# A Mamba-2 and latent-attention trunk: a planner with a DMA queue, larger transposes, and the first block's x in column halves

## The chip, the cores and the metric

The kernel runs on one core of a Trainium2 chip. The metric is the device time in microseconds of one execution of the whole program. The engines are TensorE (PE, with its weight loads PEld), VectorE (DVE), ScalarE (ACT), GpSimd (POOL) and SyncE (SP), which issues nearly all DMAs. The 16 DMA engines move what SP and POOL issue.

## The reference

Two layers on 2048 tokens of width 1024, each a pre-RMSNorm mixer with a residual add, and a final RMSNorm. Cut to what matters:

```python
h = x                                            # (1, 2048, 1024) float32
hn = rms_norm(h, g_pre[0])
z, xBC, dt = split(hn @ w_in)                    # 2048, 2048 + 2*4*128, 32 columns
xBC = silu(causal_conv4(xBC)); xs, B, C = split(xBC)
dt = softplus(dt + dt_bias); A = -exp(A_log)
y = ssd_scan(xs, dt, A, B, C)                    # 32 heads of 64, 4 groups, state 128, chunks of 256
y = group_rms((y + D * xs) * silu(z)) * g_out
h = h + y @ w_out
ckv, k_rope = split(rms_norm(h, g_kv_in) @ w_dkv)             # 256 + 32 columns
k_nope, v = split(rms_norm(ckv, g_ckv) @ w_ukv)               # 16 heads, 64 + 64
cq, gate = split(rms_norm(h, g_pre[1]) @ mla_w_in)            # 384 + 1024 columns
q = rms_norm(cq, g_q) @ w_uq                                  # 16 heads, 64 + 32 (rotary)
o = causal_softmax(q k^T) v
h = h + (o * silu(gate)) @ mla_w_out
return rms_norm(h, g_final)
```

## The kernel before

The tokens are tiled in four blocks of 512. A product of two float32 numbers is made of three products of 16-bit (or rounded 32-bit) halves, so each matrix product is issued as three matmuls per 128 rows of the contraction, into 128x512 banks of PSUM. The halves come from a copy on ACT and a subtraction on DVE.

The work comes in three stages.

1. **Mamba and MLA's projections** (to about 1960 us). `mamba` loads the constants `c_pack` (tile `pack`, 128x646, its first 128 columns the identity, behind it the gains), then block 0 of x (`load_x`: four tiles `hx` of 128x1024), squares it on ACT for the row scale (`rows_rms`, output `yt` with its sum `ms`), transposes it on PE against the identity, and splits it (`prep`: tiles `xT`, scaled by gains in `pack`). `steps` makes dt (tiles `big`, the dt chain on DVE, with the row scale `r`), `xbc` the conv inputs of a group of heads (first B and C, then the values `xs`), with weights loaded raw (`wraw`, three buffers) and split (`wsp`). Blocks 1 to 3 and MLA's blocks go through `prep16`, which scales x, splits it in 16-bit halves in `wsp` and transposes them by DMA (`DMA_TRANSPOSE xT<-wsp`, 128x8x128: eight squares of 128x128 in one). The residual is kept in `h_d` in DRAM, with tiles `hs`. MLA's part has for each block `mla_kv_down` and `mla_cq`, whose latents `turned` transposes by DMA, two squares at a time (tiles `BC` and `yT`), `mla_up` and `mla_gate`.

   All of that is not issued as it is written. It is recorded in a `Score`: each instruction with a cost from `cost()` (time on its engine, and time until its result is there), its dependencies (`graph`) and its tiles. `plan()` makes a list schedule from the front (`forward`: each engine takes, of what is ready, what has the best rank; eight DMAs of SP in flight at most), then one from the back (`backward`), which gives the ranks of the next turn, and keeps the plan with the earliest end. `play()` issues the instructions in that order. So costs and due times set the order of every engine, and also which buffer a tile gets. In the profile all these instructions stand at one line, L878 (L887 after).

2. **Attention** (about 1960 to 2600 us). `heads` issues 64 steps (head by block) from an order made by a planner with written tables, `Pace`. While it works on the last block, it begins the output product of block 0: for each of eight k, tasks G (loads of output, gate and reciprocal sums, `load_gated`, into a staging tile `os`), H (two DVE steps, L2260 and L2262), I (ACT copy of the upper half), J (DVE subtraction for the lower half, L2327) and P (products with `W`, L904 to L906). `GATED` is the number of staging tiles, `ASKED` at which of the 64 steps which k is begun.

3. **Output** (`back`, to the end). For blocks 1 to 3 the same by k in `gated`: loads into `os`, L2260, L2262, the copy to `oT` (L2466) and the subtraction (L2467). Then `residual` (L2481), `final` (L2487) and the stores.

Of the kernel before, what the change touches and what calls it, by code (L numbers as in the profile page):

```python
# [46 lines left out]
GATED = 2  # L47
ASKED = {61: (0,), 62: (1,), 63: (2, 3, 4, 5, 6)}
# [474 lines left out]
class Score:  # L523

    def __init__(self, nc, blank, name):
        self.ops, self.owns, self.rings = [], [], {}
# [103 lines left out]
    def graph(self):  # L630
# [201 lines left out]
    def plan(self):  # L832
# [48 lines left out]
class Net:  # L881
# [665 lines left out]
    def load_x(self, b, src, tag="hx"):  # L1547
# [1069 lines left out]
```

## Time and profile before

| | us |
|---|---|
| median of 3 runs | 2784.39 (2779.01 to 2787.86) |
| the profiled execution | 2791.74 |
| its span, first to last instruction | 2789.9 |
| PE busy | 2737.9 (98% of the span) |
| DVE, ACT, POOL busy | 2220.0, 1864.2, 675.6 |
| mean granted clock of PE | 0.994 |

In a row of the timeline or of the groups, `ps<-K,xT` reads output from inputs by the program's names; the numbers are start and length in us, and brackets hold the idle time before with what ended it. A granted clock of 1.00 is full speed. Busy PE is PE with a matmul in its array, at whatever clock.

### The profile page before, as it was taken

What the parts mean: (1) busy time and instruction counts of PE and PEld (TensorE: products, weight loads), DVE (VectorE), ACT (ScalarE), POOL (GpSimd) and SP (SyncE); (2) the same over time, 40 slices, a digit from 0 to 9 for tenths busy, and PEclk for the clock granted to TensorE, in tenths of its full rate; (3) what the DMA queues carried; (4) which work ended last, traced back from release to release, by engine and by line L of the source; (5) the groups of instructions that cost most, each with busy time, mean ns of one, the idle gap of its engine ahead of it and who ended that gap; (6) DMA issues with size and microseconds to landing.
All of it is one profiled execution on the core that took longest, in us unless ns stands there. A gap on an engine that the chain in (4) does not pass through costs nothing. (4 is left out here: it accounts for less than half of the span.)

```text
span 2789.9 us, 48569 instructions
## 1 busy us (share of the span) xinstructions
PE 2737.9 (98%) x16120; PEld 1550.7 (56%) x16120; DVE 2220.0 (80%) x5048; ACT 1864.2 (67%) x4914; POOL 675.6 (24%) x832
## 2 busy tenths in 40 slices
PE   7999999999999999999999999999999999999998
PEld 6888766554555555555555545454555555555443
DVE  5889899999988879888786564646889888889676
ACT  6889877877776667666655453334888888888322
POOL 0000000000000000000002121324888888888200
PEclk9999999999999999999999999999999999999999
DMA  5333456768668655586567987976999999999894
GB/s 178 98 113 105 118 178 220 215 204 256 187 187 256 175 141 178 160 243 185 145 186 232 292 236 210 250 197 183 181 189 183 186 203 198 190 200 185 209 278 153
DMA packets 687904, 535.88 MB, mean 192 GB/s; under 512 B 496642, under 2 KB 538626, under 8 KB 687652
## 3 DMA queue, kind: packets, MB, share of 16 engines
q1 hardware_dynamic: 674500, 490.16, 69.4%
q0 software_dynamic: 13152, 42.61, 5.1%
q8 instruction: 127, 2.08, 0.3%
q14 instruction: 125, 1.02, 0.1%
HBM read 307.57 MB, written 108.66 MB: 149 GB/s over the span
## 5 line engine op out<-in xcount | busy, mean ns | idle before, releaser
L878 PE MATMUL ps<-xT,wsp 128*128 128x512 f16 (+2 forms) x2416 | 567.7, 386 | 8.7 <-DVE wsp L878 6.0
L878 PE MATMUL ps<-wsp,xT 128*128 128x512 f16 (+3 forms) x2304 | 464.4, 358 | 1.9 <-DVE Sp L878 1.2
L2356 ACT ACTIVATE Pr<-ps,nm 128x512 f32<-128x512 f32 (+3 forms) x640 | 394.5, 628 | 83.7 <-DVE nm L2351 78.1
L2345 DVE TENSOR_REDUCE mx<-ps 128x1 f32<-128x512 f32 (+3 forms) x640 | 366.4, 604 | 54.1 <-PE ps L2311 45.9
L878 PEld LDWEIGHTS <-wsp 128*128 128x128 f16 x2448 | 234.0, 98 | 281.2 <-issue 21.6
L2362 POOL TENSOR_TENSOR HL<-Pr,HL 128x512 f16<-128x512 f32 x320 | 372.6, 1164 | 25.6
L878 PE MATMUL ps<-wsp,yT 128*128 128x512 f16 (+1 forms) x1536 | 356.7, 385 | 1.0 <-DVE rb L878 0.6
L878 POOL DMA_DIRECT2D gate_d<-xs x24 | 13.8, 590 | 1115.4 <-DVE kn L878 1101.3
L878 PEld LDWEIGHTS <-xT 128*128 128x128 f16 x1920 | 185.7, 98 | 166.5 <-issue 6.2
L904 PE MATMUL ps<-K,xT 96*128 96x512 f16 (+3 forms) x640 | 223.0, 348 | 2.9 <-ACT Pr L2356 1.8
L906 PE MATMUL ps<-K,xT 96*128 96x512 f16 (+3 forms) x640 | 221.9, 347 | 0.0
L905 PE MATMUL ps<-K,xT 96*128 96x512 f16 (+3 forms) x640 | 221.8, 347 | 0.0
L2361 POOL CAST HL<-Pr 128x512 f16<-128x512 f32 x320 | 196.6, 614 | 91.7 <-ACT Pr L2356 91.5
L878 DVE SCALAR_TENSOR_TENSOR cacc<-craw,pack,cacc 128x512 f32<-128x512 f32 x288 | 211.4, 746 | 4.6 <-ACT cacc L878 4.1
L878 PEld LDWEIGHTS <-yT 128*128 128x128 f16 x1152 | 110.2, 98 | 129.2 <-issue 3.8
L878 ACT ACTIVATE big<-big,d_cum 128x128 f32<-128x128 f32 x512 | 168.5, 393 | 8.8 <-DMA big<-cumT 8.8
L878 PE MATMUL ps<-xT,st 128*128 128x512 f16 x672 | 154.8, 382 | 3.7 <-DMA st<-w_d 3.7
L2375 ACT ACTIVATE PH<-ps 128x512 f16<-128x512 f32 (+3 forms) x320 | 143.4, 484 | 14.1 <-PE ps L2370 13.3
L2397 PE MATMUL ps<-PX,xT 128*64 128x512 f16 (+1 forms) x640 | 146.2, 383 | 1.6 <-DMA PX<-HL 1.2
L2397 PEld LDWEIGHTS <-xT 128*128 128x128 f16 (+1 forms) x1280 | 95.4, 103 | 91.4 <-issue 15.4
L2356 ACT ACTIVATION_READ_ACCUMULATOR Pr<-ps,nm 128x1 f32 x640 | 133.8, 209 | 0.0
L2370 PE MATMUL ps<-pack,Pr 128*128 128x128 f32 x896 | 133.4, 274 | 0.3 <-ACT Pr L2356 0.3
(380 smaller groups left out, 5348.3 us busy)
## 6 DMA issues: line engine op xcount, KB each, us to landing
wsp<-w_d SPq DMA_DIRECT2D x68, 512.0 KB, 3.9
wraw<-in_ssm_w_in_dram SPq DMA_DIRECT2D x128, 256.0 KB, 3.2
big<-cumT SPq DMA_DIRECT2D x64, 512.0 KB, 4.2
wraw<-in_ssm_w_out_dram SPq DMA_DIRECT2D x64, 256.0 KB, 3.3
w_d<-wsp SPq DMA_DIRECT2D x32, 512.0 KB, 4.3
wsp<-wo_d SPq DMA_DIRECT2D x32, 512.0 KB, 4.3
st<-w_d SPq DMA_DIRECT2D x56, 256.0 KB, 3.7
wsp<-wu_d SPq DMA_DIRECT2D x28, 512.0 KB, 4.2
```

The costliest lines, as they stand in the source:

```text
L878: call(*[self.real(x) for x in args], **{k: self.real(x) for k, x in named.items()})
L904: mm(out, l_hi, r_hi, start=start, stop=False)
L905: mm(out, l_hi, r_lo, start=False, stop=False)
L906: mm(out, l_lo, r_hi, start=False, stop=stop)
L2345: v.tensor_reduce(m[:, at:at + 1], s, AX.X, ALU.max, negate=True)
L2356: nc.scalar.activation(tile("Pr", n, j, c)[:, :w], bank("S", n, j, c)[:, :w], AF.Exp, bias=moves[(4 * n + j) % len(moves)], accum_out=sums ...
L2361: nc.gpsimd.tensor_copy(u[:, 0], x)
L2362: nc.gpsimd.tensor_tensor(u[:, 1], x, u[:, 0], ALU.subtract)
L2370: nc.tensor.transpose(bank("T", n, k)[:, j * P:(j + 1) * P], tile("Pr", n, j, k // 4)[:, k % 4 * P:(k % 4 + 1) * P], self.ident)
L2375: nc.scalar.activation(tile("PH", n, k)[:, c], bank("T", n, k)[:, c], AF.Copy)
L2397: nc.tensor.matmul(o, weights, half(n, k, low), start=start, stop=not left[n][at[0]])
```

## The change

No matmul is added, removed or altered. There are five parts:

- **The planner's model of DMAs.** A transpose was 1.4 us of issue and 3.3 until it lands, outside any queue; a copy went through a queue of 260 bytes per ns. Now both go through one queue (`wires`: 545 ns + bytes/288 for a transpose, 102 + bytes/359 for a copy), and `LATE`, added to each, is 600 for 1000 ns. The pass from the back has a queue too, and `FAR`, 1800 ns, per transfer. With `EARLY`, no row of SP is planned more than 30 us before it is due. 16 turns for 12. `links` are extra order edges.
- **Larger transposes.** `turned` transposes kv_down's latent of 256 in one DMA of four squares per 128 tokens instead of two of two; cq's 384 in one of four and one of two instead of three of two. Over four blocks there are 48 instead of 80.
- **The first block.** The identity is loaded first and the rest of `pack` behind four half tiles of x; x comes in eight DMAs of 128x512; the four squares on ACT are linked behind the fourth copy of `prep`.
- **Attention's end.** Four staging tiles for two (the new ones in parts of `K[0]` and of held tiles that are free by then), k = 0 and 1 begun at step 62 instead of 61 and 62, and H planned 7.5 instead of 5.5 us behind G.
- **The output stage.** Five buffers `os` for three.

```diff
-GATED = 2
-ASKED = {61: (0,), 62: (1,), 63: (2, 3, 4, 5, 6)}
+GATED = 4
+ASKED = {62: (0, 1), 63: (2, 3, 4, 5, 6)}
...
-                self.at(self.now + 5500, lambda k: self.ready["DVE"].append(("H", k, 0)), k)
+                self.at(self.now + 7500, lambda k: self.ready["DVE"].append(("H", k, 0)), k)
...
-PLANS = 12
+PLANS = 16
+EARLY = 30000
...
             if named.get("transpose"):
-                return 1400, 3300
-            issue = 700 if engine == "POOL" else 400
-            return issue, -moved
+                self.wires[len(self.ops)] = 545 + moved / 288
+                return 1300, 2470 + moved / 276
+            self.wires[len(self.ops)] = 102 + moved / 359
+            return 700 if engine == "POOL" else 400, 2000 + moved / 276
...
+        for m, n in self.links:
+            if all(m != k for k, _ in preds[n]):
+                preds[n].append((m, False))
...
-    SLACK, LATE = dict(DVE=40, ACT=40), 1000
+    SLACK, LATE, FAR = dict(DVE=40, ACT=40), 600, 1800
...
-        est = [0.0] * len(ops)
+        est = [max(0.0, due + rank[n] - EARLY) if o[0] == "SP" else 0.0 for n, o in enumerate(ops)]
...
-            if took < 0:
-                dma = max(dma, t) - took / 260
-                took = max(dma, t + 1900 - took / 160) - t + self.LATE
+            if n in self.wires:
+                dma = max(dma, t + 500) + self.wires[n]
+                took = max(took, dma + 1690 - t) + self.LATE
...
-            back[n] = t
...
+            if n in self.wires:
+                wire = max(wire + self.wires[n], t)
+                t = max(t, wire)
+            back[n] = t
...
-                if took_m < 0:
-                    took_m = 2400 - took_m / 150
-                elif f == "SP":
-                    took_m += 800
+                if m in self.wires:
+                    took_m += self.FAR
...
+            due = end if i > 1 else 0.0
...
-        nc.sync.dma_start(self.pack, self.a["c_pack"])
+        for cs in (slice(0, P), slice(P, PACK)):
+            nc.sync.dma_start(self.pack[:, cs], self.a["c_pack"][:, cs])
+        ops = self.score.ops
         self.load_x(0, self.a["x"][0:TB])
+        self.score.links += [(0, n) for n in range(2, 6)] + [(n, 1) for n in range(2, 6)]
+        squares = [n for n, o in enumerate(ops) if o[0] == "ACT"][:4]
...
+            if n == 0:
+                turned = [n for n in range(at, len(ops)) if ops[n][0] == "ACT"]
+                self.score.links += [(turned[3], n) for n in squares]
...
-        for i in range(4):
-            nc.sync.dma_start(xs[i], src[i * P:(i + 1) * P, :])
+        n = 1 if b else 2
+        for h in range(n):
+            cs = slice(h * D // n, (h + 1) * D // n)
+            for i in range(4):
+                nc.sync.dma_start(xs[i][:, cs], src[i * P:(i + 1) * P, cs])
...
-        out = [self.t(self.sp, tag, [P, 4, 2, P], F16, bufs=4) for _ in range(n)]
+        sets = [(k, m, self.t(self.sp, "yT" if m == 2 else "BC", [P, 4, 2 * m, P], F16, bufs=4))
+                for k, m in ((0, 2), (2, 1))[:n - 1]]
...
-            for k in range(n):
-                nc.sync.dma_start(out[k][:, i], u[:, k].rearrange("p s c -> p (s c)"), transpose=True)
-        return out
+            for k, m, o in sets:
+                nc.sync.dma_start(o[:, i], u[:, k:k + m].rearrange("p k s c -> p (k s c)"), transpose=True)
+        return [o[:, :, 2 * j:2 * j + 2] for k, m, o in sets for j in range(m)]
...
-                s = self.t(sp, "os", [P, 3, TB], bufs=3)
+                s = self.t(sp, "os", [P, 3, TB], bufs=5)
```

What the planner makes of it is shown at three places. First the start of SP's queue (`hx` and `hs` are tiles of x). Before:

```order
L878 DMA pack<-in_c_pack_dram 128x646
L878 DMA hx_139<-in_x_dram 128x1024
L878 DMA hx_148<-in_x_dram 128x1024
L878 DMA hx_150<-in_x_dram 128x1024
L878 DMA hx_152<-in_x_dram 128x1024
L878 DMA wraw_154<-in_ssm_w_in_dram 128x8x32
L878 DMA wraw_156<-in_ssm_w_in_dram 128x2x128
L878 DMA wraw_158<-in_ssm_w_in_dram 128x2x128
L878 DMA hs_160<-in_x_dram 128x1024
L878 DMA hs_169<-in_x_dram 128x1024
L878 DMA hs_182<-in_x_dram 128x1024
L878 DMA hs_202<-in_x_dram 128x1024
```

After:

```order
L887 DMA pack<-in_c_pack_dram 128x128
L887 DMA hx_141<-in_x_dram 128x512
L887 DMA hx_148<-in_x_dram 128x512
L887 DMA hx_150<-in_x_dram 128x512
L887 DMA hx_152<-in_x_dram 128x512
L887 DMA pack<-in_c_pack_dram 128x518
L887 DMA wraw_155<-in_ssm_w_in_dram 128x8x32
L887 DMA hx_141<-in_x_dram 128x512
L887 DMA hx_148<-in_x_dram 128x512
L887 DMA wraw_160<-in_ssm_w_in_dram 128x2x128
L887 DMA hx_150<-in_x_dram 128x512
L887 DMA hx_152<-in_x_dram 128x512
```

The four `hs` loads, and four `hx` of block 1 that came behind them, are gone from here; weights follow instead. On DVE at the same place, the subtractions that finish the weights of B and C (`wsp`, eight of 128x256) and the dt chain (`big`). Before, the chain's last part, with the third to sixth subtraction in it and behind it:

```order
L878 TENSOR_TENSOR wsp_365<-wraw_251,wsp_365 128x256
L878 TENSOR_SCALAR big_330<-big_330 128x128
L878 TENSOR_TENSOR big_330<-big_330 128x128
L878 TENSOR_TENSOR wsp_370<-wraw_287,wsp_370 128x256
L878 TENSOR_SCALAR big_330<-big_330 128x128
L878 TENSOR_TENSOR wsp_380<-wraw_299,wsp_380 128x256
L878 TENSOR_TENSOR big_330<-big_330 128x128
L878 SCALAR_TENSOR_TENSOR d_dt_399<-big_330 128x128
L878 TENSOR_TENSOR big_330<-d_dt_399,pack 128x128
L878 TENSOR_TENSOR wsp_412<-wraw_378,wsp_412 128x256
```

After, the last two of the eight and the head of the chain:

```order
L887 TENSOR_TENSOR wsp_340<-wraw_292,wsp_340 128x256
L887 TENSOR_TENSOR rss_365<-rsy_357 128x4
L887 SCALAR_TENSOR_TENSOR rsq_370<-rsx_335,rss_365 128x4
L887 TENSOR_TENSOR wsp_359<-wraw_305,wsp_359 128x256
L887 SCALAR_TENSOR_TENSOR rsy_375<-rsq_370,rsy_357 128x4
L887 TENSOR_TENSOR rss_380<-rsy_375 128x4
L887 SCALAR_TENSOR_TENSOR rsq_383<-rsx_335,rss_380 128x4
L887 SCALAR_TENSOR_TENSOR rsy_388<-rsq_383,rsy_375 128x4
L887 COPY r_106<-rsy_388 128x4
L887 TENSOR_SCALAR rh_107<-rsy_388 128x4
L887 SCALAR_TENSOR_TENSOR big_394<-ps_345,r_106,pack 128x32 x2
```

The chain's first step stood ahead of the third subtraction before; now it stands behind the eighth. Second, SP in MLA's first block, where the transposes of the next block's x (`xT<-wsp`) meet the residual (`h_d`, `hs`). Before:

```order
L878 DMA h_d<-hs_13842 128x1024
L878 DMA h_d<-hs_13855 128x1024
L878 DMA wsp_17563<-wu_d 128x1024
L878 DMA hs_17569<-h_d 128x1024
L878 DMA hs_17573<-h_d 128x1024
L878 DMA Xd_17579<-in_mla_w_out_dram 128x512
L878 DMA Xd_17589<-in_mla_w_out_dram 128x512
L878 DMA hs_17620<-h_d 128x1024
L878 DMA hs_17644<-h_d 128x1024
L878 DMA_TRANSPOSE xT_17407<-wsp_17614 128x8x128
L878 DMA_TRANSPOSE xT_17407<-wsp_17626 128x8x128
```

After:

```order
L887 DMA_TRANSPOSE xT_17322<-wsp_17301 128x8x128
L887 DMA_TRANSPOSE xT_17334<-wsp_17301 128x8x128
L887 DMA wsp_17347<-wu_d 128x2x1024
L887 DMA_TRANSPOSE xT_17322<-wsp_17314 128x8x128
L887 DMA_TRANSPOSE xT_17334<-wsp_17314 128x8x128
L887 DMA_TRANSPOSE xT_17322<-wsp_17272 128x8x128
L887 DMA wsp_17381<-wu_d 128x1024
L887 DMA_TRANSPOSE xT_17334<-wsp_17272 128x8x128
L887 DMA st_3157_17407<-w_d 128x1024
L887 DMA st_3160_17415<-w_d 128x1024
L887 DMA h_d<-hs_14129 128x1024
```

Six of the eight transposes now stand ahead of the first of these stores; the other two follow it, and the loads `hs` come behind all eight. Third, DVE in the output stage of block 1, where `final` of block 0 (the four wide `h`) meets the gates of k = 6 and 7. Before:

```order
L1338 SCALAR_TENSOR_TENSOR rsy_4128_29911<-rsq_4127_29909,rsy_4125_29905 128x4
L2487 SCALAR_TENSOR_TENSOR h_29804<-h_29804,rsy_4128_29911,gf 128x1024
L2487 SCALAR_TENSOR_TENSOR h_29805<-h_29805,rsy_4128_29911,gf 128x1024
L2487 SCALAR_TENSOR_TENSOR h_29806<-h_29806,rsy_4128_29911,gf 128x1024
L2487 SCALAR_TENSOR_TENSOR h_29807<-h_29807,rsy_4128_29911,gf 128x1024
L2260 TENSOR_TENSOR os_29921<-os_29921 128x512
L2260 TENSOR_TENSOR os_29931<-os_29931 128x512
L2262 SCALAR_TENSOR_TENSOR os_29921<-os_29921,us 128x512
L2262 SCALAR_TENSOR_TENSOR os_29931<-os_29931,us 128x512
L2467 TENSOR_TENSOR oT_29928<-os_29921,oT_29928 128x512
L2467 TENSOR_TENSOR oT_29938<-os_29931,oT_29938 128x512
```

After:

```order
L2492 TENSOR_TENSOR oT_29893<-os_29886,oT_29893 128x512
L1343 TENSOR_TENSOR rss_4115_29866<-rsy_4114_29864 128x4
L1345 SCALAR_TENSOR_TENSOR rsq_4116_29868<-rsx_4109_29854,rss_4115_29866 128x4
L1347 SCALAR_TENSOR_TENSOR rsy_4117_29870<-rsq_4116_29868,rsy_4114_29864 128x4
L1343 TENSOR_TENSOR rss_4118_29872<-rsy_4117_29870 128x4
L2281 TENSOR_TENSOR os_29896<-os_29896 128x512
L1345 SCALAR_TENSOR_TENSOR rsq_4119_29874<-rsx_4109_29854,rss_4118_29872 128x4
L2283 SCALAR_TENSOR_TENSOR os_29896<-os_29896,us 128x512
L1347 SCALAR_TENSOR_TENSOR rsy_4120_29876<-rsq_4119_29874,rsy_4117_29870 128x4
L2512 SCALAR_TENSOR_TENSOR h_29769<-h_29769,rsy_4120_29876,gf 128x1024
L2512 SCALAR_TENSOR_TENSOR h_29770<-h_29770,rsy_4120_29876,gf 128x1024
```

The gate of k = 6 (`oT_29893`) is whole ahead of the wide rows, and of k = 7 only the subtraction stands behind them.

More of the change, by code (lines that the diff above doesn't have):

```diff
@@ L693, in graph, with forward @@
             o.roots = [n for n in o.ops if not any(m in inside for m, _ in preds[n])]
-    SLACK, LATE = dict(DVE=40, ACT=40), 1000
+    SLACK, LATE, FAR = dict(DVE=40, ACT=40), 600, 1800
     HEAR = dict(PE=52, DVE=36, ACT=36, POOL=90, SP=60)
-    def forward(self, rank, order):
+    def forward(self, rank, order, due):
         ops, preds, succs, uses = self.ops, self.preds, self.succs, self.uses
         left = [len(p) + len(u) for p, u in zip(preds, uses)]
-        est = [0.0] * len(ops)
+        est = [max(0.0, due + rank[n] - EARLY) if o[0] == "SP" else 0.0 for n, o in enumerate(ops)]
         start = [0.0] * len(ops)
@@ L732, in forward @@
             if not k:
-                heapq.heappush(waiting[ops[n][0]], (0.0, n))
+                heapq.heappush(waiting[ops[n][0]], (est[n], n))
+                heapq.heappush(events, (est[n], ops[n][0]))
         for o in order:
@@ L796, in backward @@
         events = []
+        wire = 0.0
         for n, k in enumerate(left):
@@ L838, in plan @@
         order = sorted(self.owns, key=lambda o: o.first)
-        best = None
+        best, due = None, 0.0
         for i in range(PLANS):
-            made = self.forward(rank, order)
+            made = self.forward(rank, order, due)
             if made is None:
@@ L1453, in mamba @@
         self.r0, self.rh0 = cp.tile([P, 4], F32, name="r0"), cp.tile([P, 4], F32, name="rh0")
-        nc.sync.dma_start(self.pack, self.a["c_pack"])
+        for cs in (slice(0, P), slice(P, PACK)):
+            nc.sync.dma_start(self.pack[:, cs], self.a["c_pack"][:, cs])
+        ops = self.score.ops
         self.load_x(0, self.a["x"][0:TB])
+        self.score.links += [(0, n) for n in range(2, 6)] + [(n, 1) for n in range(2, 6)]
+        squares = [n for n, o in enumerate(ops) if o[0] == "ACT"][:4]
         self.layer_constants(cp)
-        for part in (self.prep(0, self.g0), self.steps(0), self.xbc(0, 0), self.zgate(0, 0)):
+        at = len(ops)
+        for n, part in enumerate((self.prep(0, self.g0), self.steps(0), self.xbc(0, 0), self.zgate(0, 0))):
             for _ in part:
                 pass
+            if n == 0:
+                turned = [n for n in range(at, len(ops)) if ops[n][0] == "ACT"]
+                self.score.links += [(turned[3], n) for n in squares]
         for n, (b, g) in enumerate(items):
@@ L2098, in mla_cq @@
         yield
-        self.qT += self.turned(raw, f, 3, "yT")
+        self.qT += self.turned(raw, f, 3)
         for k in range(3):
@@ L2267, in attention @@
             self.W = [self.t(self.wo, f"W{k}", [P, 2, 2, TB], F16, bufs=1) for k in range(KD)]
-            self.staged = [self.t(self.wo, f"os{k}", [P, 3, TB], bufs=1) for k in range(GATED)]
+            staged = [self.t(self.wo, f"os{k}", [P, 3, TB], bufs=1) for k in range(2)]
+            staged = [[s[:, i] for i in range(3)] for s in staged]
+            free = [self.K[0][:, i // 2, i % 2 * 1024:i % 2 * 1024 + 1024] for i in range(4)]
+            free += [self.held(i)[:, 2 * j:2 * j + 2].rearrange("p a b -> p (a b)") for i in (3, 4) for j in range(2)]
+            free = [x.bitcast(F32) for x in free]
+            self.staged = staged + [free[0:3], free[4:7]]
             places = [self.K[0][:, 2 + i // 2, i % 2 * 1024:i % 2 * 1024 + 1024].rearrange(
@@ L2313, in staged @@
         def staged(k):
-            s = self.staged[slot[("st", k)]]
-            return s[:, 0], s[:, 1], s[:, 2]
+            return self.staged[slot[("st", k)]]
         def G(k, i):
```

6 lines of the change are left out of this document (3 added, 3 removed).

## The prediction

> **What bounds the kernel now.** I read the page's busy times first, then the windows by stage, PE's waits, PE's timeline at those waits, and last the engines that it waits for.
>
> ```profile
> PE 2737.9 (98%) x16120; PEld 1550.7 (56%) x16120; DVE 2220.0 (80%) x5048; ACT 1864.2 (67%) x4914; POOL 675.6 (24%) x832
> PE   7999999999999999999999999999999999999998
> ```
>
> TensorE is the bound, and no matmul is taken away. All that can be won lies in the 2789.9 − 2737.9 = 52.0 us without PE work and in matmuls at a slow clock. The windows by stage say where (columns: width, then busy time of PE, PEld, DVE, ACT, POOL, then granted clock, DMA share, GB/s):
>
> ```profile
> 0.00:70.00 70.00, 54.66 (x230) 42.41 (x230) 39.44 (x105) 44.33 (x119) 0.20 (x4) 0.93 0.55 179
> 70.00:1540.00 1470.00, 1469.00 (x8827) 854.64 (x8826) 1258.07 (x2744) 1052.41 (x2753) 22.30 (x33) 1.00 0.63 180
> 1540.00:1960.00 420.00, 405.54 (x2109) 205.80 (x2108) 235.01 (x528) 183.67 (x361) 117.43 (x166) 0.99 0.82 228
> 1960.00:2520.00 560.00, 558.44 (x3676) 327.26 (x3675) 494.19 (x1265) 475.58 (x1411) 463.85 (x551) 1.00 1.02 191
> 2520.00:2781.00 261.00, 250.28 (x1287) 120.62 (x1285) 189.70 (x396) 106.73 (x271) 71.77 (x80) 0.99 0.82 212
> 2781.00:2789.90 8.90, 0.02 (x1) 0.00 (x0) 3.56 (x15) 1.44 (x3) 0.00 (x0) 0.65 0.15 59
> ```
>
> Idle PE: 15.3 us in the start, 1.0 in the Mamba stage, 14.5 in MLA's projections, 1.6 in attention, 10.7 in the tail, and 8.9 behind the last matmul, which the change leaves alone. Behind a long wait the granted clock is 0.50 for a while:
>
> ```profile
> 1568.60:1572.00 3.40, 3.40 (x9) 1.19 (x9) 3.40 (x7) 0.69 (x2) 2.65 (x4) 0.50 1.02 333
> 1800.70:1807.50 6.80, 5.82 (x14) 2.09 (x15) 6.10 (x13) 1.38 (x2) 2.02 (x4) 0.50 0.89 268
> 2667.70:2671.10 3.40, 2.93 (x7) 1.00 (x8) 1.77 (x3) 1.05 (x2) 0.00 (x0) 0.50 1.04 260
> ```
>
> Half of the busy time there is loss too: 1.7 + 2.9 us in MLA (19.1 with its idle time), 1.5 in the tail (12.2). PE's longest waits (total, times, longest):
>
> ```profile
> PE ps L878 <- DMA hx<-in_x_dram: 6.6, 2, 5.6
> PE ps L878 <- DVE wsp L878: 6.0, 2, 4.1
> PE ps L904 <- ACT oT L2466: 5.9, 2, 4.1
> PE ps L878 <- DVE yT L878: 4.5, 1, 4.5
> PE ps L878 <- DMA st<-w_d: 3.7, 1, 3.7
> ...
> PE ps L906 <- DVE xT L2327: 2.0, 1, 2.0
> ```
>
> **The change, part by part. The first block.** PE at the start (start, length, group, wait):
>
> ```profile
> 5.63 1.09 PE L878 MATMUL ps<-pack,hx 128*128 128x128 f32 x4 [5.63 <-DMA hx<-in_x_dram]
> 7.72 5.40 PE L878 MATMUL ps<-pack,hx 128*128 128x128 f32 x28 [1.00 <-DMA hx<-in_x_dram]
> 30.91 6.07 PE L878 MATMUL ps<-xT,wsp 128*128 128x512 f32 x15 [4.10 <-DVE wsp L878]
> 43.56 22.66 PE L878 MATMUL ps<-xT,wsp 128*128 128x512 f32 x96 [1.69 <-ACT wsp L878]
> ```
>
> From 43.56, the first value projection, PE runs unbroken; how much earlier that group starts is the gain. ScalarE, whose copies of the transposed x all projections need:
>
> ```profile
> 5.52 1.06 ACT L878 ACTIVATE yt<-hx 128x1024 bf16<-128x1024 f32 x1 [1.01 <-DMA hx<-in_x_dram]
> 6.49 0.19 ACT L878 ACTIVATION_READ_ACCUMULATOR yt<-hx 128x1 f32 x1
> 12.40 1.27 ACT L878 ACTIVATE xT<-ps,pack 128x512 fp32r<-128x512 f32 x2 [0.69 <-PE ps L878]
> 13.86 3.00 ACT L878 ACTIVATE xT<-ps,pack 128x512 fp32r<-128x512 f32 x5
> 25.39 1.02 ACT L878 ACTIVATE wsp<-wraw 128x256 fp32r<-128x256 f32 x3
> ```
>
> and what the transfers carried:
>
> ```profile
> 0.00:5.00 5.00, 0.00 (x0) 0.00 (x0) 0.97 (x10) 1.91 (x5) 0.20 (x4) 1.00 0.64 202
> 5.00:10.00 5.00, 3.37 (x15) 3.00 (x16) 0.00 (x0) 3.23 (x5) 0.00 (x0) 1.00 1.05 348
> 5.00:45.00 40.00, 29.66 (x120) 22.25 (x121) 22.41 (x70) 20.55 (x54) 0.00 (x0) 0.87 0.58 200
> 25.00:30.00 5.00, 0.96 (x3) 0.48 (x3) 4.39 (x15) 2.20 (x10) 0.00 (x0) 0.92 0.00 0
> 30.00:35.00 5.00, 4.09 (x10) 3.26 (x11) 3.27 (x12) 0.82 (x3) 0.00 (x0) 0.50 0.31 82
> ```
>
> The first copy needs the identity (0.066 MB), four half tiles (1.05 MB) and the rest of the constants, which hold the gains (0.265 MB): 1.38 MB. The old transfers had carried 202 x 5 = 1.01 MB by 5.0 us; the other 0.37 MB at 348 GB/s take 1.1, so it can start at about 6.4 instead of 12.40. The four squares are no longer ahead of it. The 4 MB of x for later use (hs, second hx) have left SP's first rows (the plan issues a transfer at most 30 us before it is due, four times the 7.4 that such a load took, quoted below), and all eight subtractions of B and C weights now precede the dt chain on VectorE, in which the window 25 to 30 had 4.39 us of VectorE, 0.96 of PE and no transfer at all, since the reloads wait for those subtractions. That is the 4.10 us wait, and the 0.50 clock after it.
>
> What remains is a sum of work. ScalarE from 6.4: eight copies of 0.60 (3.00/5), eight weight tiles of two 0.34 (1.02/3) and a read-out of 0.19, 7.0, four squares of 1.06 + 0.19, 5.0, and one 0.34 for the dt weights: 17.1, so 23.5. PE from about 5.2: 29.66 less the 1.44 after 43.56 is 28.2 busy, which at the mean clock of 0.87 is 24.6 at full clock, so 29.8: PE ends last. The value projection then starts between 28.8 (some dt matmuls, 1 us, put off) and 33.4 (the slow stretches remain: 5.2 + 28.2), against 43.56: a gain of 10.2 to 14.8. PE begins between copies of 0.60, not back to back, so I take 12; a copy that waits for the constants widens it to 8 to 15. The halves and the split constants are five issues more on SP, which cost 0.43 each at the median:
>
> ```profile
> L878 SPq DMA_DIRECT2D hx<-in_x_dram x16: 327/426/738, 1.2 to 953.1; - x16
> ```
>
> The six that the first copy needs take 2.6 us of issue and hide behind 5 us of transfer; without that cover they would cost those 2.6. Late next is the row scale, which waits for the squares and so for ScalarE's end at 23.5: the dt chain and the scaling of B and C stand behind it on VectorE, but TensorE uses neither before its chunk sums, well into the value projection's 22.66 us.
>
> **MLA's transposes.** SP's issue times (least, median, longest, ns):
>
> ```profile
> L878 SPq DMA_TRANSPOSE yT<-yt x96: 1167/1244/2873, 465.7 to 1871.2; - x96
> L878 SPq DMA_TRANSPOSE xT<-wsp x56: 1237/1384/5407, 333.8 to 1794.6; - x56
> L878 SPq DMA_TRANSPOSE BC<-yt x32: 1173/1231/2028, 1475.9 to 1851.2; - x32
> ```
>
> yT and BC move two 128x128 squares each, xT eight, and the issue differs by 0.14 us. So 32 fewer small ones free 32 x 1.24 = 39.7 us of SP. A merged one waits for nothing more, since both of its parts are written by the same two instructions; of its four squares the issue lies between 1.24 and 1.38, and I take 1.24, the nearer size. It is no gain by itself: PE stalls only where a transfer or a copy behind them is late. [...]
>
> **The planner in MLA.** Two rows, SP's and VectorE's, at the longest stall (PE idle until 1568.52):
>
> ```profile
> 1554.49 10.62 SPq L878 DMA_TRANSPOSE xT<-wsp  x4
> 1565.55 0.88 DVE L878 TENSOR_SCALAR xT<-xT,xg 128x1024 f16<-128x1024 f16 x2 [5.80 <-DMA xT<-wsp]
> ```
>
> The next block's four transposes stood behind stores and loads of the residual; VectorE idled 5.80 us at the head of its queue, with the evacuation that PE needed behind. Now six of the eight stand ahead of the first store and all ahead of the loads. I count this stall (4.5 + 1.7 slow clock) as gone. Of the other 12.9 us in MLA I take 1.8: the largest, st (3.7 + 2.9), waits for a transfer behind xT transposes whose issue does not change. That is −8; ends 0 (new waits of the same size) and −15.
>
> **Attention's end and the tail.** Four staging slots and a later scaling (7.5 for 5.5 us) take the first block's gates from in front of late transfers; the 2.0 us wait for xT may go. In block 1:
>
> ```profile
> 2660.72 4.87 DVE L2487 SCALAR_TENSOR_TENSOR h<-h,rsy,gf 128x1024 f32<-128x1024 f32 x4
> ```
>
> Gates k = 6 and 7 stood behind these four; PE waited 4.1 and lost 1.5 to the clock. Now k = 6 is complete before them and covers 24 matmuls (3 products, 8 banks) at 0.19 to 0.24 us (250.28/1287 in the tail's window, with narrower ones among them; 22.66/96 at the start, in the slower type): 4.7 to 5.7 us, about the 4.87 that it has to hide. Of 5.6 + 2.0 + 1.8 (the second oT wait) I take 5, since this cover is only just enough; ends +2 and −9. With os buffers 3 to 5 the loads of two more gates may be under way; the window's DMA share of 0.82 leaves them room.
>
> **The rest of the plan.** From 70 to 1540 and 1960 to 2520 there are only 2.6 us to win, and a new order of every engine can lose. The old plan gave a lone 512 KB load 1.9 + 3.3 + 1.0 = 6.2 us, the new one 2.0 + 1.9 + 0.6 = 4.5 (worked out from the diff: 524,288 bytes over 160, and over 276). The trace:
>
> ```profile
> wsp<-w_d SPq DMA_DIRECT2D x68, 512.0 KB, 3.9
> hs<-in_x_dram SPq DMA_DIRECT2D x16, 512.0 KB, 7.4
> ```
>
> A load that lands at its median of 3.9 is covered; one that takes 7.4 is not, by 2.9, unless the shared queue, which now counts transposes, foresaw it. I take +3 (one such wait); ends 0 and +12 (four).
>
> **Sum:** −12 −8 −5 +3 = −22. Against the profiled execution's 2791.74 (span 2789.9 and 1.84 around it) that is 2769.7. That execution is 7.35 above the median of 2784.39; on the median's scale it is 2762.
>
> **Rivals.**
> *The start alone.* MLA and tail give as many new waits as they lose. For it: the plan is a new draw, and st waits on transfers of unchanged length. Against: two stalls have a visible cause that the orders remove. −12, 2772.
> *The first block stays slow.* With the clock at 0.50 through B and C (30 to 35 shows it), PE's 24.6 us of work take up to 12 more, and the start gains nothing: −8 −5 +3 = −10, 2774. Against: it was at 1.00 from 5 to 10 and the waits get shorter.
> [...]
> *Given back.* Five to nine new waits of 2.9 us in the Mamba stage, with the gains of 25 standing: −25 + 14.5 to −25 + 26, 2774 to 2785, and 2780 in the middle.
> *Slower.* The tighter allowance in 1470 us of full PE decides: each 512 KB load that lands at 7.4 where 4.5 was planned costs 2.9, and 1.7 more where the clock falls. Against 25 us of gains it needs 12 such waits (34.8) to be 10 slower, 2794. Against: the old plan had 1.0 us of waits there in all, and 3.9 is the usual landing.
>
> **How the numbers follow.** Chances: the sum as it stands 0.50 (2750 to 2771), start alone 0.17, slow first block 0.08, transposes by the square 0.03, given back 0.13, slower 0.06, more than 34 us gained 0.03. What a measurement here tells from no change is 0.3%, 8.4 us: 2776.0 and 2792.8. Of start alone and slow first block, a fifth (0.05) lies above 2776; so does nearly all of given back. Faster 0.76, same 0.18, slower 0.06. The range 2747 to 2780 leaves out slower, half of given back and most of the best case, under 0.17.
>
> **What would show it.** Right: value projection's first matmul at 29 to 33 instead of 43.56; the first xT copy near 6.5; 48 yT/BC transposes in MLA at 1.2 us each; PE idle under 8 us in MLA's windows; no wait on oT above 1 us. Wrong: transposes at 2.4 us; a clock of 0.5 between 8 and 28 us; PE below 1460 of 1470 in the Mamba windows, with waits on DMA or on wsp. If the Mamba stage loses over 12 us, the planner's allowance was my error; if the start gains under 8, ScalarE's or PE's chain there was.

## The result, and the profile after

The changed kernel takes 2767.44 us (median of 4 runs, 2764.32 to 2772.73) against 2785.11 for the kernel before (4 runs): ratio 0.9937, 95% interval 0.9914 to 0.9960. That is 17.7 us faster, with 11 to 24 in the interval; 22 had been forecast, and 2762. The profiled execution took 2772.73, with a span of 2770.9; it is the slowest of the four, as the profiled one of before (2791.74) lies above its four. Its busy times and PE's 40 slices:

```profile
PE 2732.5 (99%) x16120; PEld 1549.5 (56%) x16120; DVE 2216.7 (80%) x5048; ACT 1869.1 (67%) x4914; POOL 674.1 (24%) x832
PE   9999999999999999999999999999999999999898
```

The first slice, 7 before, is 9 now. The windows by stage (columns as in the prediction), after:

```profile
0.00:70.00 70.00, 64.54 (x287) 51.84 (x288) 50.12 (x126) 53.50 (x147) 0.20 (x4) 1.00 0.48 137
70.00:1470.00 1400.00, 1399.83 (x8506) 818.23 (x8505) 1203.94 (x2616) 1018.31 (x2666) 2.87 (x5) 1.00 0.61 179
1470.00:1960.00 490.00, 473.85 (x2456) 239.00 (x2455) 287.11 (x658) 224.28 (x450) 147.97 (x207) 0.99 0.88 236
1960.00:2520.00 560.00, 559.27 (x3676) 326.71 (x3674) 495.98 (x1268) 474.60 (x1412) 464.08 (x551) 1.00 1.02 191
2520.00:2762.00 242.00, 234.66 (x1204) 113.76 (x1202) 175.97 (x367) 96.92 (x239) 58.98 (x67) 0.99 0.83 219
```

and of the kernel before, the two stages that are divided at 1470 here:

```profile
70.00:1470.00 1400.00, 1399.00 (x8479) 820.68 (x8478) 1215.79 (x2634) 1019.27 (x2685) 4.12 (x7) 1.00 0.62 178
1470.00:1960.00 490.00, 475.54 (x2457) 239.76 (x2456) 277.29 (x637) 216.81 (x431) 135.61 (x192) 0.99 0.81 227
```

| idle PE, us | before | after |
|---|---|---|
| start (0 to 70) | 15.3 | 5.5 |
| Mamba (70 to 1470) | 1.0 | 0.2 |
| MLA's projections (1470 to 1960) | 14.5 | 16.2 |
| attention (to 2520) | 1.6 | 0.7 |
| tail (to the last matmul) | 10.7 | 7.3 |
| behind the last matmul | 8.9 | 8.6 |
| sum | 52.0 | 38.5 |

The span fell by 19.0: 13.5 of idle time and 5.4 of busy time, for the same matmuls run less often at the slow clock (busy 2737.9 to 2732.5, mean granted clock 0.994 to 0.996). In the start the clock rose from 0.93 to 1.00. PE's longest waits now:

```profile
PE ps L887 <- DMA st<-w_d: 10.6, 3, 6.0
PE ps L887 <- DMA hx<-in_x_dram: 5.5, 3, 4.3
PE ps L2422 <- DMA PX<-HL: 2.8, 3, 1.2
PE ps L887 <- DVE xs L887: 2.3, 1, 2.3
```

The waits on VectorE's wsp and yT and on ScalarE's oT, 16.4 us in all before, are gone. The wait on st has grown from 3.7 to 10.6. The timeline's start on PE:

```profile
4.25 1.08 PE L887 MATMUL ps<-pack,hx 128*128 128x128 f32 x4 [4.25 <-DMA hx<-in_x_dram]
13.90 10.96 PE L887 MATMUL ps<-xT,wsp 128*64 128x512 f32 x46
28.89 23.11 PE L887 MATMUL ps<-xT,wsp 128*128 128x512 f32 x98
```

and ScalarE's first copy:

```profile
8.00 0.69 ACT L887 ACTIVATE xT<-ps,pack 128x512 fp32r<-128x512 f32 x1 [5.58 <-DMA pack<-in_c_pack_dram]
```

The group at 28.89 is two matmuls of B and C and the 96 of the value projection, which so starts near 29.4 instead of 43.56. The first copy waits for the constants until 8.00.

### The profile page after: what moved, and what is told of

Its sections match the earlier page's. It is cut to its first block, busy times and chain, and to the rows that moved or that the text cites. A ratio compares the mean times of both kernels' runs of the same rounds, so it can differ in the third digit from the quotient of the medians.

```text
span 2770.9 us, 48519 instructions
## 1 busy us (share of the span) xinstructions
PE 2732.5 (99%) x16120; PEld 1549.5 (56%) x16120; DVE 2216.7 (80%) x5048; ACT 1869.1 (67%) x4914; POOL 674.1 (24%) x832
## 5 line engine op out<-in xcount | busy, mean ns | idle before, releaser
L887 PE MATMUL ps<-wsp,yT 128*128 128x512 f16 (+1 forms) x1728 | 400.0, 384 | 0.0
L887 POOL DMA_DIRECT2D gate_d<-xs x24 | 13.5, 565 | 1124.9 <-DVE xs L887 1118.1
L887 PEld LDWEIGHTS <-yT 128*128 128x128 f16 x1344 | 129.2, 98 | 151.2 <-issue 3.5
L887 PE MATMUL ps<-xT,st 128*128 128x512 f16 x672 | 156.2, 383 | 10.6 <-DMA st<-w_d 10.6
```

Of the source, the lines that this page charges most:

```text
L887: call(*[self.real(x) for x in args], **{k: self.real(x) for k, x in named.items()})
```

## The experiments

All were timed against the kernel before on the same chip, unless it says one execution; e1 to e4, e5 to e8, e9 to e11 and e12 each ran on another chip, so that runs of different groups are compared by their ratios to before. "Before" and "changed" are the two kernels of the case. Any edit to what the planner sees lets it make a new plan for the stages before 1960 us.

**The parts alone (e1 to e4).** e1 is the kernel before with only this:

```diff
+        for cs in (slice(0, P), slice(P, PACK)):
+            nc.sync.dma_start(self.pack[:, cs], self.a["c_pack"][:, cs])
...
+        self.score.links += [(0, n) for n in range(2, 6)] + [(n, 1) for n in range(2, 6)]
...
+                self.score.links += [(turned[3], n) for n in squares]
...
+        n = 1 if b else 2
+        for h in range(n):
+            cs = slice(h * D // n, (h + 1) * D // n)
+            for i in range(4):
+                nc.sync.dma_start(xs[i][:, cs], src[i * P:(i + 1) * P, cs])
```

> The kernel before with the first block's edit alone (constants split, x in half columns, squares behind the fourth copy), under the old planner. Theory A, the parts add up and the start belongs to this edit: the unbroken value projection starts near 31 us instead of 43.56, so -12 us, ratio 0.9957. Rival B, the planner makes the start (it moves the weights' subtractions ahead of the dt chain and the later x out of SP's first rows): this edit alone brings the first copy from 12.4 to about 8 us but the 4 us wait for wsp and the slow clock stay, so -4 to -6 us, ratio 0.998.

Measured: ratio 0.9991 (0.9980 to 1.0003), 0.5 us by the medians. Its start and MLA:

```profile
0.00:70.00 70.00, 57.90 (x251) 43.60 (x252) 44.29 (x112) 48.98 (x134) 0.20 (x4) 0.98 0.59 184
1470.00:1960.00 490.00, 471.01 (x2427) 236.67 (x2426) 274.96 (x621) 213.21 (x419) 136.26 (x193) 0.99 0.82 226
```

In the start it wins 3.2 us of idle PE and some slow clock (0.93 to 0.98), and the first copy comes at 8.53: rival B for the start. The longest wait for wsp, which B left standing at 4 us, is 1.7. B's 4 to 6 us of the whole time are at the very edge of the interval (a gain of 5.6 to a loss of 0.8); MLA idles 4.5 us more in this execution (19.0 against 14.5). e2 is the kernel before with only the new planner:

```diff
-            if took < 0:
-                dma = max(dma, t) - took / 260
-                took = max(dma, t + 1900 - took / 160) - t + self.LATE
+            if n in self.wires:
+                dma = max(dma, t + 500) + self.wires[n]
+                took = max(took, dma + 1690 - t) + self.LATE
...
+        est = [max(0.0, due + rank[n] - EARLY) if o[0] == "SP" else 0.0 for n, o in enumerate(ops)]
```

> The kernel before with the new planner's model alone. Theory A (start belongs to the first block's edit, MLA's stalls are only moved): -1 to +2 us, ratio 0.9996 to 1.0007. Rival B (the planner makes the start): -7 to -9 us with the value projection starting near 36 us, ratio 0.997. Rival C, the smaller allowance costs in the Mamba stage: +3 to +12 us, with PE waits on DMA between 70 and 1540 us.

Measured: ratio 0.9969 (0.9957 to 0.9980), 8.6 us. Its start and the Mamba stage:

```profile
0.00:70.00 70.00, 61.97 (x275) 49.66 (x276) 49.45 (x128) 52.95 (x142) 0.20 (x4) 0.98 0.46 136
70.00:1470.00 1400.00, 1400.00 (x8497) 819.18 (x8496) 1203.38 (x2614) 1015.56 (x2664) 3.09 (x5) 1.00 0.61 179
```

Rival B holds: with whole x tiles, the constants in one piece and the squares unlinked, the planner alone takes 7.3 of the 9.9 us by which PE's idle time in the start fell. Which part of it does this, the queue, the allowances or the limit of 30 us, e2 doesn't separate. Rival C falls for the Mamba stage, which lost nothing by the smaller allowance; but in MLA this plan's longest wait is on just such a 512 KB load (wsp from `w_d`, 11.3 us in two waits).

e3 is the kernel before with only the larger transposes (`turned` as in the change).

> The kernel before with the larger transposes alone. Theory A (issue time is flat, SP gets 39.7 us, but MLA's stalls are late transfers in a full DMA queue and not SP's issue): within 3 us of before. Rival B (SP's issue is what delays MLA): PE's idle time between 1540 and 1960 falls from 14.5 us to under 8, -6 to -9 us. Rival C (a transpose of four squares takes twice the issue of two): median issue about 2.4 us, within 1 us of before.

Measured: ratio 1.0050 (1.0032 to 1.0068), 14 us slower (17.6 by the medians), which no theory had. Its waits:

```profile
PE ps L878 <- DMA st<-w_d: 8.7, 2, 4.6
PE ps L878 <- DVE BC L878: 4.7, 2, 4.4
```

and its windows of Mamba and MLA:

```profile
70.00:1470.00 1400.00, 1395.62 (x8451) 818.89 (x8450) 1210.26 (x2626) 1016.73 (x2677) 3.95 (x7) 1.00 0.61 177
1470.00:1960.00 490.00, 469.53 (x2412) 236.16 (x2410) 266.89 (x618) 206.62 (x404) 122.71 (x178) 0.98 0.81 226
```

MLA idles 20.5 us. Mamba idles 4.4, and there nothing was edited but the plan is new. So the old planner's new plan accounts for at least the 3.4 us in Mamba; whether the larger transposes cost anything in MLA by themselves under the old planner stays open (under the new one e5 tells).

e4 is the kernel before with only attention's end and the output stage:

```diff
-GATED = 2
-ASKED = {61: (0,), 62: (1,), 63: (2, 3, 4, 5, 6)}
+GATED = 4
+ASKED = {62: (0, 1), 63: (2, 3, 4, 5, 6)}
...
-                s = self.t(sp, "os", [P, 3, TB], bufs=3)
+                s = self.t(sp, "os", [P, 3, TB], bufs=5)
```

> The kernel before with attention's end and the output stage alone (four staging tiles, first gates at step 62, scaling 7.5 us behind the loads, five os buffers). The recorded stages before 1960 us keep their plan to the row. Theory A: the two waits on oT (5.9 us) and the slow clock behind go, about -5.5 us, ratio 0.998. Rival B: the tail's gain came from where the new plan left the transfers, and this alone gives under 2 us.

Measured: ratio 0.9968 (0.9954 to 0.9982), 8.9 us, 5 to 13 in the interval. MLA and the tail:

```profile
1470.00:1960.00 490.00, 478.96 (x2499) 242.42 (x2499) 282.04 (x651) 221.74 (x444) 139.71 (x198) 1.00 0.81 230
2520.00:2768.10 248.10, 241.96 (x1246) 116.63 (x1240) 181.15 (x380) 101.84 (x254) 65.02 (x73) 0.99 0.86 218
```

The tail idles 6.1 us against 10.7, and no wait on oT is left: theory A, with the low end of its interval. The first row matters as much. Up to 1960 us this kernel issues the same instructions in the same order on every engine as the kernel before, and yet MLA idles 11.0 us in this execution and 14.5 in the other. So one execution's MLA is no measure of an edit to a few us.

**Parts taken out of the changed kernel (e5, e7, e8).** e5 has the small transposes again (`turned` of before).

> The changed kernel with the small transposes of before (80 instead of 48), all else as changed. Theory A (the larger transposes are worth nothing, and e3's loss is a plan that came out worse for them): within 4 us of the changed kernel, 2764 to 2772, PE's idle time between 1470 and 1960 within its spread of 15 to 23. Rival B (they cost by themselves, since a later block waits for the whole of them: 14 us alone): 2755 to 2760, faster than the changed kernel by 8 or more. Rival C (under the new planner SP's 39.7 us count): 2775 or more.

Measured: 2771.96 us, ratio to before 0.9941 (0.9923 to 0.9960) where the changed kernel has 0.9937 (0.9914 to 0.9960). The larger transposes are worth nothing that this can tell. That is theory A; a gain of 8 us without them (B) isn't seen, and C's time isn't reached, but the intervals are 10 and 13 us wide, so that a few us either way stay open. e7 has whole x tiles, e8 no link that holds the squares back:

```diff
-        n = 1 if b else 2
+        n = 1
```

> The changed kernel with block 0's x in four whole tiles again; identity first, rest of the constants behind x, squares behind the fourth copy. Theory A (half columns let the first copy start early, and SP's order does the rest): first copy 1 to 2 us later than 8.0, value projection's start 1 to 2 us later than in the changed kernel. Rival B (PE's work from the first transpose on bounds the start): the same to 0.5 us.

```diff
-                self.score.links += [(turned[3], n) for n in squares]
+                pass
```

> The changed kernel without the link that holds the four squares behind the fourth copy. Theory A: the planner puts the squares where ScalarE would idle, the start within 1 us of the changed kernel. Rival B: they come first, 4 x 1.25 us ahead of the first copies, and the value projection starts 3 to 5 us later.

Measured, one execution each: 2760.46 and 2764.56. The start's window of e7:

```profile
0.00:70.00 70.00, 61.90 (x278) 48.93 (x279) 49.99 (x127) 52.62 (x144) 0.20 (x4) 0.98 0.46 136
```

and of e8:

```profile
0.00:70.00 70.00, 63.49 (x281) 50.34 (x282) 49.94 (x126) 52.45 (x142) 0.20 (x4) 0.98 0.47 137
```

Against 64.54: the halves are worth 2.6 us of PE's time in the start. That is theory A in kind, a little larger: the first copy of e7 came at 10.86, 2.9 us later. The link's 1 us can't be told from nothing, as e5, e6, e9 and e10, which have the first block's edit whole, show 63.32 to 63.96 in this window; so theory A for the link too. The totals, 2760.46 and 2764.56, lie below the changed kernel's profiled 2772.73 by MLA again: it idles 6.6 us in e7's execution and 10.4 in e8's. e7's kernel, timed:

> The changed kernel with block 0's x in whole tiles again, timed; its one execution took 2760.46 us with 9 us lost in MLA, although its start lost 2.5 us more. Theory A (a lucky plan in MLA that lasts over executions): 2758 to 2763, faster than the changed kernel by about 7. Rival B (that execution was at the good end of its spread): 2765 to 2771.

Measured: 2766.10 us (2760.19 to 2768.53), ratio to before 0.9916 (0.9897 to 0.9934). Rival B: the execution at 2760 was at the good end of the spread. This gives two traces of one and the same program, e7's and e11's, and their rows of MLA:

```profile
1470.00:1960.00 490.00, 483.36 (x2549) 246.59 (x2547) 298.39 (x688) 234.89 (x485) 154.68 (x216) 1.00 0.87 240
1470.00:1960.00 490.00, 479.49 (x2521) 244.27 (x2519) 294.24 (x676) 230.89 (x474) 151.02 (x212) 1.00 0.87 238
```

Idle 6.6 and 10.5 us. In e11 PE waits 5.4 us on st once; in e7 that wait isn't among its longest. In the start e11 has 61.29 us of PE, so the halves are worth 2.6 to 3.3.

**What MLA waits for (e6, e9, e10, e12).** In the changed kernel, SP and PE around the longest wait:

```profile
1638.87 3.30 SPq L887 DMA_DIRECT2D st<-w_d  x2
1642.22 2.15 SPq L887 DMA_DIRECT2D Xd<-in_mla_w_out_dram  x1
1644.42 9.77 SPq L887 DMA_TRANSPOSE xT<-wsp  x2
...
1652.33 5.88 PE L887 MATMUL ps<-xT,st 128*128 128x512 f16 x20 [5.97 <-DMA st<-w_d]
```

The load of st was issued at 1638.87 and PE got it at 1652.3, 13.4 us later, where such a load lands in 4.5 at the median. The two transposes that took 9.77 us to issue stand behind it on SP, so their issue didn't hold this load up (one ahead of it, 5.40 us of issue from 1633.38, may have): it and they were slow together. From 1645 to 1650 the DMA engines moved 103 GB/s at a share of 1.04, ten us later 293 at 1.08 (columns as above, the last two are DMA share and GB/s):

```profile
1645.00:1650.00 5.00, 1.36 (x7) 0.39 (x4) 0.57 (x1) 0.00 (x0) 0.00 (x0) 1.00 1.04 103
1655.00:1660.00 5.00, 5.00 (x25) 2.17 (x24) 4.62 (x12) 3.04 (x5) 1.28 (x2) 0.98 1.08 293
```

e6 doubles a transpose's time in the planner's queue:

```diff
-                self.wires[len(self.ops)] = 545 + moved / 288
+                self.wires[len(self.ops)] = 1090 + moved / 144
```

> The changed kernel with the planner's transposes at twice the time in its DMA queue (1090 ns + bytes/144). Theory A (MLA's waits on st come from a queue that the planner believes emptier than it is, SP's transposes then taking 4 to 7 us of issue): the three waits on st (10.6 us) fall under 4, 2757 to 2762. Rival B (the waits come from st's place in SP's order, whatever the cost): PE waits on st or on another load of the same size, 2764 to 2772.

Measured: 2774.91 us, ratio to before 0.9960 (0.9943 to 0.9976). The waits on st are gone, but in the list of waits one of 11.5 us took their place:

```profile
PE ps L887 <- DVE Sp L887: 11.5, 1, 11.5
```

and its timeline has, on SP, a single transpose that took 13.29 us to issue:

```profile
1777.27 13.29 SPq L887 DMA_TRANSPOSE xT<-wsp  x1
```

VectorE waited 7.30 us for this block's transposes, and 2.28 us more, for something that the trace doesn't name, ahead of the next rows on them, with the evacuations that PE needed behind:

```profile
1797.66 1.68 DVE L887 TENSOR_SCALAR xT<-xT,xg 128x1024 f16<-128x1024 f16 x4 [7.30 <-DMA xT<-wsp]
1802.28 0.88 DVE L887 TENSOR_SCALAR xT<-xT,xg 128x1024 f16<-128x1024 f16 x2 [2.28 <-issue]
```

Theory A falls in its time and B in its wait and time: the planner's cost moves the wait, the slow transpose stays, and 2774.91 is outside both. Counting in the first ten traces (before, after, e1 to e8) how many of GpSimd's DMAs were in flight when a transpose was issued between 1400 and 1960 us (issued before it, landed after its issue began):

| GpSimd DMAs in flight | 0 | 1 | 2 | 3 | 4 | 5 | 6 | 7 | 8 |
|---|---|---|---|---|---|---|---|---|---|
| transposes | 472 | 145 | 227 | 134 | 55 | 26 | 13 | 6 | 3 |
| median issue, us | 1.23 | 1.24 | 1.26 | 1.50 | 2.13 | 2.67 | 4.28 | 4.87 | 8.90 |
| over 3 us | 11 | 5 | 17 | 16 | 13 | 10 | 8 | 5 | 3 |

Slow transposes and GpSimd's DMAs that pile up go together; which is the cause the table can't say. Three things limit it. It mixes transposes of two to eight squares; of the eight-square ones alone the medians are 1.64, 1.34, 1.55, 2.43, 3.34, 4.23 and 4.53 us with 0 to 6 in flight. Of the 31 of these with none in flight 9 took over 3 us, up to 7.93, so GpSimd isn't the only cause. And not all that it counts are stores: three of the five in flight at the transpose of 13.29 us were attention's first loads of `K`. e9 issues MLA's stores from ScalarE (two of four such lines):

```diff
-            nc.gpsimd.dma_start(d[:, :, t0:t0 + TB], u)
+            nc.scalar.dma_start(d[:, :, t0:t0 + TB], u)
...
-                    nc.gpsimd.dma_start(self.v_d[h0:h0 + 8, :, 4 * b + i].rearrange("h p d -> p h d"),
+                    nc.scalar.dma_start(self.v_d[h0:h0 + 8, :, 4 * b + i].rearrange("h p d -> p h d"),
```

> The changed kernel with MLA's stores of keys, values, queries and gates (DMAs issued from GpSimd before) issued from ScalarE instead. In the traces so far the issue of a transpose in MLA has a median of 1.23 us with no GpSimd store in flight, 2.1 with four and 4.3 with six. Theory A (GpSimd's stores, as software-made DMAs, hold the transposes up): hardly a transpose in MLA above 3 us, PE's idle time between 1470 and 1960 below 9 us, 2755 to 2760. Rival B (any store does it, the engines are shared): transposes of 4 us and more remain where several stores are in flight, and the time stays within 2763 to 2772. Rival C: a store waiting at the head of ScalarE's queue holds up copies behind it, PE waits on ACT, 2775 or more.

Measured: 2762.59 us (2760.98 to 2766.45), ratio to before 0.9910 (0.9892 to 0.9927). SP's transposes in MLA (least, median, longest, ns), in the changed kernel:

```profile
L887 SPq DMA_TRANSPOSE xT<-wsp x24: 1238/2208/6783, 1513.9 to 1783.7; - x24
```

in e9:

```profile
L887 SPq DMA_TRANSPOSE xT<-wsp x24: 1233/1706/3573, 1511.2 to 1775.1; - x24
```

and e9's window of MLA:

```profile
1470.00:1960.00 490.00, 482.78 (x2539) 246.25 (x2537) 295.19 (x686) 232.96 (x480) 54.62 (x75) 1.00 0.88 239
```

Theory A by the transposes: none is above 3.6 us, and 4 of the 24 take over 3 us, where each of the twelve traces with GpSimd's stores has 7 to 11 and a longest of 4.2 to 13.3. The idle time of 7.2 us says little, since e7 idled 6.6 with GpSimd's stores. The time lies between A's and B's. GpSimd was busy for 147.97 of MLA's 490 us in the changed kernel (its DMA issues not counted), and the longest transpose issue on SP fell from 6.78 to 3.57 us. The issuer isn't all that changed, as the queues show (packets, MB, share of the 16 engines), in the changed kernel:

```profile
q0 software_dynamic: 13152, 42.61, 5.1%
```

and in e9:

```profile
q10 hardware_dynamic: 58880, 35.92, 4.6%
q0 software_dynamic: 2016, 6.69, 0.8%
```

The same 35.9 MB go through another kind of queue and in packets of 0.6 KB at the mean, not 3.2. And rival B's condition, several stores in flight, can't be counted here: the profile tells the landing of only about half of ScalarE's stores.

e10 is the changed kernel with the planner's second best plan, not its best:

```diff
-            if best is None or end < best[0]:
+            if i != 8 and (best is None or end < best[0]):
```

> The changed kernel with the planner's second best plan (another of its 16 turns, 124 of SP's 1643 rows stand elsewhere) and not one line of the computation altered. Theory A (what MLA loses is set by which of many nearly equal plans is played, not by the edits): the time differs from the changed kernel by 4 us or more, in either direction, all of it between 1470 and 1960 us. Rival B (plans of nearly equal planned end run alike): within 3 us of it, 2764 to 2770.

Measured: 2766.90 us, runs from 2759.92 to 2771.39, ratio to before 0.9923 (0.9902 to 0.9945). Rival B, for this one pair of plans: the median is within 1 us of the changed kernel's, the ratio 4 us lower with the intervals overlapping. The spread of 11.5 us is one program's, and its MLA, with GpSimd's stores and this plan, idles 8.3 us in an execution of 2760.78:

```profile
1470.00:1960.00 490.00, 481.70 (x2531) 245.05 (x2529) 297.28 (x688) 232.96 (x475) 154.17 (x215) 1.00 0.88 240
```

e9's six runs span 5.5 us, e11's, of the same group, 8.3.

e12 moves the stores in the kernel before.

> The kernel before with MLA's stores of keys, values, queries and gates issued from ScalarE, nothing else changed but what its planner makes of that. Theory A (GpSimd's stores hold the transposes up and this is what MLA loses most of its time to): longest transpose issue in MLA under 4 us, PE's idle time between 1470 and 1960 under 10 us against 14.5, 4 to 8 us faster than before, ratio 0.997 to 0.9985. Rival B (e9's 5 us came with its plan): within 3 us of before.

Measured: ratio 0.9985 (0.9972 to 0.9998), 4.2 us by the ratio, 3.2 by the medians. The same row of transposes, in the kernel before and in e12:

```profile
L878 SPq DMA_TRANSPOSE xT<-wsp x24: 1237/1750/5407, 1522.1 to 1794.6; - x24
L878 SPq DMA_TRANSPOSE xT<-wsp x24: 1237/1614/3845, 1527.8 to 1793.3; - x24
```

and its windows of MLA and Mamba:

```profile
1470.00:1960.00 490.00, 481.85 (x2531) 245.49 (x2530) 281.37 (x651) 222.54 (x447) 40.37 (x58) 1.00 0.85 233
70.00:1470.00 1400.00, 1394.46 (x8433) 816.83 (x8432) 1212.21 (x2632) 1016.11 (x2676) 1.36 (x3) 1.00 0.60 177
```

Theory A for the transposes under a second planner: the longest takes 3.8 us for 5.4, and 3 of 24 take over 3 us for 7. MLA idles 8.1 us for 14.5 (11.0 in e4, which has the same order as before). But the old planner's new plan now idles 5.5 us in the Mamba stage, for 1.0, and that eats most of it. That GpSimd's stores make transposes slow is supported by both kernels (longest issue 6.78 to 3.57 us in one, 5.41 to 3.85 in the other). Each has a new plan besides, but no plan of the other twelve traces has so few slow ones. Whether by their queue, their larger packets or their number in flight do it is open, and so is how much of MLA's time hangs on it.

e9 has the lowest ratio of all kernels timed. It is faster than the kernel before by 20 to 30 us. Against the changed kernel it is 4.9 us by the medians, and against e10 and e11 on its own chip 4.3 and 3.5, but the intervals overlap: that it is faster than these isn't shown.

## Why the prediction was right, point by point

The sum, −22, against −17.7, and 2762 against 2767.44, inside the range. Of its four terms two held, and two were wrong in opposite directions. By the two profiled executions the terms came out at about −14 (start, from 43.56 to 29.4), +2 (MLA), −5 (tail, 3.4 of idle time and some 1.5 of slow clock) and −2 (the rest), −19 in all. So the total is partly luck: MLA missed by 10 us, and the start and the rest made good 7 of them.

- **The start, −12: right in size.** Idle time −9.9 and the slow clock gone (0.93 to 1.00); the value projection at 29.4, where 28.8 to 33.4 had been worked out and 31.6 taken. Two steps inside were off. The first copy came at 8.00, not 6.4 (5.0 + 1.1, the step's own terms, make 6.1): the constants are the last of its 1.38 MB, and the first 5 us carried 145 GB/s, not the 202 that I had taken over from whole tiles:

```profile
0.00:5.00 5.00, 0.75 (x4) 0.71 (x4) 0.50 (x5) 1.68 (x4) 0.20 (x4) 1.00 0.58 145
5.00:45.00 40.00, 38.79 (x173) 30.65 (x172) 28.84 (x81) 30.91 (x83) 0.00 (x0) 1.00 0.50 142
```

  That cost at most the 1.2 us that PE then idled up to 45 us, because PE's sum of work ends last, as the step said: 38.79 of 40 us busy, at full clock. And the step gave the edit of the first block as its heading; alone that wins 3.2 us of idle time (e1), the planner alone 7.3 (e2). What the prediction listed beside the halves, the later x out of SP's first rows and the subtractions ahead of the dt chain, comes with the planner and was the larger part; which of the two counts more isn't shown.
- **The transposes, nothing by themselves: right.** 48 instead of 80 in MLA, with the issue of the larger ones where it was taken:

```profile
L887 SPq DMA_TRANSPOSE yT<-yt x32: 1190/1202/2623, 1470.1 to 1855.6; - x32
L887 SPq DMA_TRANSPOSE BC<-yt x16: 1230/1246/2412, 1483.5 to 1857.1; - x16
```

  The 32 have four squares each, the 16 have two. An issue that grows by the square, to which the prediction's chances give 0.03, is shown by no run: the medians here are 1.20 us for four squares and 1.25 for two, and the least of the eight-square ones in MLA is 1.24. One reading under this step was off: half of the 96 yT transposes of before are Mamba's, which move eight squares (`two[:, c % 2]`, 128x8x128), not two. MLA's 48, of two squares, have the same median of 1244 ns, so nothing hung on it. e5 finds no gain or loss under the new planner.
- **MLA, −8: wrong, +1.7 of idle time.** The step that failed: "I count this stall (4.5 + 1.7 slow clock) as gone", with nothing put in its place. The stall is gone (no wait on yT), but waits on st grew by 6.9. The prediction had the order on SP as the reason, which the planner can move; the traces show transposes whose issue swells from 1.2 to over 6 us, and a load beside them that lands after 13.4, while the DMA engines move 103 GB/s at a share of 1.04. The median of the eight-square ones in MLA even rose, 1.75 us before, 2.21 after. In e6 the new plan only changed who waited: 11.5 us on an evacuation (`Sp`) for 10.6 on st. Its end of 0, "new waits of the same size", was the case. One execution can't carry this alone: the same order gave 14.5 and 11.0, and one program 6.6 and 10.5. But if the start's −14, the tail's −5 and the rest's −2 hold, the interval of the timed runs (a gain of 11 to 24) leaves MLA between −3 and +10, an estimate that leaves out −8 too. Why the transposes swell is open but for GpSimd's part in it.
- **Attention's end and the tail, −5: right.** Idle 10.7 to 7.3, no wait on oT, and no slow clock behind one (1.00 from 2595 to 2760); e4 alone gives 8.9 (5 to 13), of which its trace shows 4.6 of idle time in the tail. The gate of k = 6 covers the four wide rows of `final`, as worked out.
- **The rest of the plan, +3: wrong, about −2.** Mamba 1.0 to 0.2, attention 1.6 to 0.7. The allowance of 4.5 us for a lone 512 KB load cost nothing in Mamba (also 0.0 in e2), though e2's plan waits 11.3 us on such loads in MLA. The rivals "given back" and "slower" rested on that and fall. Where Mamba did idle 3.4 to 4.5 us more than before, it was the old planner in two cases (e3, e12), and the new one only with its transposes doubled (e6).

The rival "the start alone" (2772) had MLA right, new waits for old ones, but not the tail, whose gain is real.

## What to carry to other kernels

Look at a planner's first rows. Here the better model of the DMAs moved loads that nobody needed yet out of the way, and was worth more than the hand edit of the same place (7.3 us of idle time against 3.2). Moving transfers in the order may only move the wait, as it did here in MLA (DMA share 0.88; 10.6 us on st became 11.5 on an evacuation in e6); look for what makes them slow, here, as e9 and e12 support, in part stores from GpSimd that pile up beside transposes (longest issue 6.78 us with them, 3.57 with the stores on ScalarE). Before a few us of a stage are explained, run the same order twice: here its idle time differed by 3.5 and 3.9 us, and the whole by up to 16 in 26 runs of the kernel before.

## What the runs showed of the hardware that I had not expected

- A DMA share of 1.04 went with 103 GB/s, and one of 1.08 with 293, ten us apart in one kernel: the share did not tell how much was moved.
- The issue of an eight-square transpose is 1.23 us at best and rose to 13.29 in one place (e6). Its median rises with the number of GpSimd's DMAs in flight from two on (1.55, 2.43, 3.34, 4.23 us with two to five); with MLA's stores issued from ScalarE the longest in MLA was 3.57 (e9) and 3.85 (e12).
- The same stores are 3.2 KB a packet at the mean when GpSimd issues them, and 0.6 KB when ScalarE does.
